# Hybrid decoder layer on one core: branch gates and projections turned token-major, seven-product pairs in gates and output projection, a normalised operand, one set of slots

## The chip, the core and the metric

The kernel runs on one NeuronCore of one Trainium2 chip. The time is device microseconds of one execution. The core has five engines with queues of their own, each worked off in order: TensorE (PE, matmuls; its weight loads are shown as PEld), VectorE (DVE), ScalarE (ACT), GpSimd (POOL) and SyncE (SP, which here only issues transfers). Matmul results land in PSUM accumulators, operands lie in SBUF, weights come from memory by DMA.

## The reference

One layer of a causal decoder, 256 tokens, width 2048, all in float32:

```python
h  = rmsnorm(x, norm1_g)
z  = h @ w_in                    # FoX q,k,v,forget; mLSTM q,k,v,o,i,f; gates ga, gm
a_out = forgetting_attention(rmsnorm(fq), rmsnorm(fk), fv, log_sigmoid(ff + bias))  # 8 heads of 128
m_out = rmsnorm(mlstm_chunkwise(mq, mk, mv, mi, log_sigmoid(mf))) * sigmoid(mo)     # 4 heads
merged = sigmoid(ga) * (a_out @ w_proj_a) + sigmoid(gm) * (m_out @ w_proj_m)
x  = x + merged @ w_out
h2 = rmsnorm(x, norm2_g)
u  = causal_dwconv3(h2 @ w_up)   # 2 x 5632 channels
x  = x + (silu(u_gate) * u_val) @ w_down
```

## The kernel before

Every product is made of three matmuls in a rounded float32 format: an operand is split into a rounded high half and the rest (`put` for activations, `wh`/`wl` for weights), and high x high, low x high and high x low are added up in PSUM. The weights stream through: SP loads chunks of 1 MB into three `raw` buffers (`load_chunk`, L106), ACT rounds half a chunk (a "sub") into `wh` (L138), DVE subtracts it into `wl` (L139), three buffers of each. `next_sub` hands out the next sub and prepares one or two ahead.

Products come in two forms. `block_b` (token-major) keeps 128 tokens x 512 channels in an accumulator: the activation block is the stationary operand, 512 weight columns move; per k-tile and per 128 tokens three matmuls of 512 columns. `block_a` (channel-major) keeps 128 channels x 512: the weight block is stationary and the activation moves, high and low halves side by side in one 512-wide matmul, then a 256-wide one for `wl`; `halves_added` then adds the two halves of the accumulator.

The stages follow each other on PE: `mog` (forget, input and output gates of the heads; three column blocks, mog0 and mog1 together in four accumulators of the pool `acc`, mog2 in the pool `aux`), `fq`, `fk`, `fv`, `mq`, `mk`, `mv`, the branch gates `g`, the projections `p`, `wo`, `up`, and w_down (accumulators `q` and `p`). `mog` to `g` multiply hT, the input times norm1_g only; the norm factor r1 (one number per token) is found while mog2 runs and is applied to the results, as a scale in token-major blocks and as a row tile `rb` in channel-major ones. `gate_evac` (L332, L336) empties the mog accumulators: sums for the gates on DVE, the sigmoid of the output gate into `og` on ACT. `g` and `p` are channel-major, so p's output can be split into the operand mT directly; `wo` is token-major.

w_down already uses pairs of k-tiles as 2x2 blocks: a plain pair ("p") is 8 block products of 3 matmuls, a pair "S" needs 7, for which DVE forms sums of weight blocks (`sums`, L123, L130, L133) and of activation blocks (`sv`, L729 to L732), and results are combined at the end (L811).

Small work (norms, attention steps) stands in a list `tasks`, which the blocks call between subs; the framework then sets the final order on each engine. The scratch `pools` matter for this change: a tile waits until its slot is free. Before, SBUF had eight slots of 8 KB (`a8`), three of 16 KB (`r16`) and one of 8 KB for `og`.

## Time and profile before

| | before |
|---|---|
| runs, median of 3 | 1405.78 us (1405.47 to 1405.92) |
| the profiled execution | 1395.04 us, span 1393.3 us |
| PE / PEld busy | 1384.7 / 1188.5 us (99% / 85%) |
| DVE / ACT / POOL busy | 995.3 / 759.1 / 60.1 us (71% / 54% / 4%) |
| memory traffic | 274.2 MB, 197 GB/s mean |
| g stage to its end, in the chain | until 487.76 us |
| p stage | 487.76 to 576.50 us |
| up stage begins | 666.49 us |

The span runs from the first instruction to the last; the profiled execution's time is a little longer. Busy shares are means over stages with different limits. The chain of waits is followed back from the last instruction; what stands in it sets the end, and what does not is hidden behind it. A row of the groups of instructions reads: line, engine, operation, output<-inputs, shapes, count | busy us, mean ns of one | idle time before them and who ended it. A row of the timeline or the chain starts with its start and its length in us. A row of the windows reads: stretch, length, then busy us and count for PE, PEld, DVE, ACT, POOL, granted PE clock, DMA share, GB/s.

### The profile page before, as it was taken

To read this page: it belongs to the slowest core of one execution; us is meant where nothing else is said; L and a number is where in the kernel's file an instruction comes from. 1 tells how busy PE (TensorE), PEld (TensorE's weight loads), DVE (VectorE), ACT (ScalarE), POOL (GpSimd) and SP (SyncE) were. 2 spreads that over 40 slices of the span, in tenths; PEclk is the share of its full clock that TensorE was granted. 3 is DMA by queue.
4 is the path that set the end of the run, shared out by engine and by line. 5 is a ranking of instruction groups with operands and counts; after the bars stand their busy time and mean duration, and the time that the engine had idled before them with its cause. 6 is when DMAs were issued, how large, how long until landed. Compare 5 with 4: busy or idle time off the path is not lost.

```text
span 1393.3 us, 19175 instructions
## 1 busy us (share of the span) xinstructions
PE 1384.7 (99%) x7347; PEld 1188.5 (85%) x7347; DVE 995.3 (71%) x1448; ACT 759.1 (54%) x1122; POOL 60.1 (4%) x92
## 2 busy tenths in 40 slices
PE   9999999999999999999999999999999999999998
PEld 8988888888888888888888888888888887878877
DVE  8556555556655577655788888888888877886886
ACT  7655544456644455555655565655656554653553
POOL 7001000000000011100000000000000000000000
PEclk9999999999999999999999999999999999999999
DMA  7645554444555555555555555555555657557553
GB/s 259 234 157 189 191 189 152 153 176 150 219 193 197 182 185 201 189 212 197 196 196 196 193 199 209 191 192 203 211 193 183 242 191 268 215 183 269 204 190 121
DMA packets 42491, 274.20 MB, mean 197 GB/s; under 512 B 4832, under 2 KB 4848, under 8 KB 11552
## 3 DMA queue, kind: packets, MB, share of 16 engines
q1 hardware_dynamic: 39168, 260.20, 52.2%
q0 software_dynamic: 3088, 12.77, 2.4%
q8 instruction: 57, 0.93, 0.3%
q14 instruction: 34, 0.28, 0.1%
q10 hardware_dynamic: 144, 0.02, 0.0%
HBM read 265.63 MB, written 7.34 MB: 196 GB/s over the span
## 4 chain that ended last, share of the span: by engine, by line
PE 98%; DMA 1%; DVE 1%; ACT 0%; issue 0%; POOL 0%; DVEq 0%; ACTq 0%
PE up L178 35%; PE q L178 12%; PE g L178 12%; PE p L178 10%; PE wo L178 6%; PE mog L178 3%; PE fq L178 3%; PE mv L178 3%; PE fk L178 3%; PE fv L178 3%; PE mk L178 2%; PE mq L178 2%; DMA raw<-in_w_dn 1%; PE ps_s L178 1%; PE ps_o L178 0%; PE ps_n L178 0%
## 5 line engine op out<-in xcount | busy, mean ns | idle before, releaser
L138 ACT ACTIVATE wh<-raw 128x1024 fp32r<-128x1024 f32 (+2 forms) x496 | 512.2, 1033 | 539.2 <-PE up L178 120.6
L139 DVE TENSOR_TENSOR wl<-raw,wh 128x1024 fp32r<-128x1024 f32 (+2 forms) x496 | 590.1, 1197 | 296.2 <-ACT wh L138 291.3
L178 PE MATMUL up<-h,wh 128*128 128x512 f32 x1408 | 488.6, 392 | 0.0
L178 PE MATMUL up<-h,wl 128*128 128x256 f32 x1408 | 394.8, 281 | 0.0
L178 PEld LDWEIGHTS up<-h,wh 128*128 128x128 f32 x1408 | 263.5, 187 | 57.3 <-DVE h L168 0.2
L178 PEld LDWEIGHTS up<-h,wl 128*128 128x128 f32 x1408 | 266.7, 189 | 0.1
L178 PE MATMUL g<-hT,wh 128*128 128x512 f32 x512 | 180.0, 397 | 0.0
L178 PE MATMUL q<-wh,ghl 128*128 128x512 f32 x512 | 156.3, 390 | 0.0
L178 PE MATMUL g<-hT,wl 128*128 128x256 f32 x512 | 142.5, 278 | 0.0
L178 PEld LDWEIGHTS g<-hT,wh 128*128 128x128 f32 x512 | 96.1, 188 | 21.7
L178 PEld LDWEIGHTS q<-wh,ghl 128*128 128x128 f32 x512 | 96.1, 188 | 20.2
L178 PE MATMUL q<-wl,ghl 128*128 128x512 f32 x256 | 97.9, 391 | 0.6 <-DVE wl L139 0.6
L178 PEld LDWEIGHTS g<-hT,wl 128*128 128x128 f32 x512 | 96.4, 188 | 0.1
L178 PE MATMUL p<-am,wh 128*128 128x512 f32 x256 | 88.8, 394 | 0.0
L703 DVE SCALAR_TENSOR_TENSOR t<-u,cst,t 128x256 f32<-128x256 f32 x176 | 84.8, 482 | 3.7 <-ACT t L701 0.7
L178 PE MATMUL wo<-wh,mT 128*128 128x512 f32 x256 | 79.5, 392 | 0.0
L178 PE MATMUL p<-am,wl 128*128 128x256 f32 x256 | 71.1, 278 | 0.0
L178 PEld LDWEIGHTS p<-am,wh 128*128 128x128 f32 x256 | 48.0, 188 | 11.1
L178 PEld LDWEIGHTS q<-wl,ghl 128*128 128x128 f32 x256 | 47.4, 188 | 11.9 <-DVE wl L139 1.4
L139 DVE TENSOR_TENSOR wl<-sums,wh 128x1024 fp32r<-128x1024 f32 x32 | 39.1, 1223 | 24.7 <-ACT wh L138 24.7
L178 PEld LDWEIGHTS wo<-wh,mT 128*128 128x128 f32 x256 | 47.6, 188 | 9.6
L138 ACT ACTIVATE wh<-sums 128x1024 fp32r<-128x1024 f32 x32 | 33.9, 1061 | 38.2 <-PE q L178 38.2
(237 smaller groups left out, 1655.4 us busy)
## 6 DMA issues: line engine op xcount, KB each, us to landing
raw<-in_w_up SPq DMA_DIRECT2D x88, 1024.0 KB, 4.8
raw<-in_w_dn SPq DMA_DIRECT2D x44, 1024.0 KB, 4.8
raw<-in_w_g SPq DMA_DIRECT2D x32, 1024.0 KB, 4.8
raw<-in_w_fox SPq DMA_DIRECT2D x24, 1024.0 KB, 4.8
raw<-in_w_p SPq DMA_DIRECT2D x16, 1024.0 KB, 4.8
raw<-in_w_out SPq DMA_DIRECT2D x16, 1024.0 KB, 4.8
raw<-in_w_mqk SPq DMA_DIRECT2D x8, 1024.0 KB, 4.8
raw<-in_w_mv SPq DMA_DIRECT2D x8, 1024.0 KB, 4.8
```

The source lines that it names most:

```text
L138: nc.scalar.activation(wh[:, :n], src, AF.Copy)
L139: nc.vector.tensor_tensor(wl[:, :n], src, wh[:, :n].bitcast(F32), ALU.subtract)
L178: nc.tensor.matmul(out, lhsT, rhs, start=start, stop=stop)
L703: nc.vector.scalar_tensor_tensor(out=t, in0=u[:, i : i + S], scalar=w[i], in1=t, op0=ALU.mult, op1=ALU.add)
```

## The change

- hT is used by `mog` only. A second operand hN, the input times norm1_g times `rb`, is made in eight tasks `normalised` (two k-tiles each), issued in the mog2 block and all of them before `gate_evac`. `fq` to `g` multiply hN, and the factor r1 or `rb` falls away from their results. For three pairs of k-tiles the tasks also make the activation sums of the S pairs (`gs`).
- `g` is token-major: four blocks of 1024 columns, the first plain, the other three with three S pairs of eight (`s_block`, which w_down now uses too). The results of the S products are combined in `late` steps, two per sub; the sigmoid is taken block by block.
- `p` is token-major; DVE multiplies by the gates and adds. The sums are then turned by transposes (`merged_pair`), split into mT, and for two pairs the activation sums of `wo` are made.
- `wo` is two blocks of 1024 columns with two S pairs of eight. The transposes of x2 for `h2` stand after the second block; the first two `up` blocks are taken in halves.
- The attention outputs are split when they are made; all large tiles come from 15 slots of 8 KB; `up` accumulates in `aux`; the accumulators of w_down swap pools accordingly.

The core of the diff:

```diff
+PLAIN = "p" * 8
+G_PAIRS = "pSpSpSpp"
+WO_PAIRS = "pSpSpppp"
...
+    def a8(name, shape, dtype=F32):
+        return big.tile([P, *shape], dtype, tag="a8", bufs=15, name=name)
...
+    add_pairs(a["w_g"], [PLAIN] + [G_PAIRS] * 3)
+    add_b(a["w_p"], 512)
+    add_pairs(a["w_out"], [WO_PAIRS] * 2)
+    n = len(subs_of)
+    add_b(a["w_up"], 512)
+    subs_of[n + 1], subs_of[n + 2] = subs_of[n + 2], subs_of[n + 1]
...
+    def put_pair(pair, src):
+
+        put(pair[:, :, 0, :], pair[:, :, 1, :], src.rearrange("p (k s) -> p k s", k=2))
+
+    def put_sums(src, dst, keep):
+
+
+
+        a11, a21, a12, a22 = (src[:, i * P : (i + 1) * P] for i in range(4))
+        n = 4 if keep else 3
+        sv = scratch("sv", [P, n * P])
+        s2, s3, s4 = (sv[:, i * P : (i + 1) * P] for i in range(3))
+        s1 = sv[:, 3 * P :] if keep else a21
+        nc.vector.tensor_tensor(s3, a21, a11, ALU.subtract)
+        nc.vector.tensor_tensor(s1, a21, a22, ALU.add)
+        nc.vector.tensor_tensor(s2, s1, a11, ALU.subtract)
+        nc.vector.tensor_tensor(s4, a12, s2, ALU.subtract)
+        put(dst[0], dst[1], sv)
...
+    def s_block(name, pairs, s_ops, pattern, pools, dst, add=True, per_piece=0):
+
+
+        q = [[pools[0](f"{name}q{tok}{h}") for h in range(2)] for tok in range(2)]
+        ps, late, left = {}, [], pattern.count("S")
+        n_s = left
...
+        def piece():
+            w = next_sub(3)
+            for _ in range(min(2, len(late))):
+                late.pop(0)()
+            run_tasks(per_piece)
+            return w
+
+        def tt(o, x, y):
+            late.append(lambda: nc.vector.tensor_tensor(o, x, y, ALU.add))
...
+            s1, s2, s3, s4 = s_ops[m]
+            w = piece()
+            prod(ps[1], op(0, 0), w, 0, first, last)
+            prod(q[0][1], s4, w, 1, False, False)
+            prod(q[0][0], op(1, 0), piece(), 0, False, False)
+            w = piece()
+            prod(ps[5], s1, w, 0, first, last)
+            prod(ps[7], s3, w, 1, first, last)
+            w = piece()
+            prod(ps[6], s2, w, 0, first, last)
+            prod(q[1][0], op(1, 1), w, 1, False, False)
...
+                late.append(lambda: nc.scalar.activation(c11, ps[1], AF.Copy))
+                tt(u2, c11, ps[6])
+                tt(c21, u2, ps[7])
+                tt(c12, u2, ps[5])
+                tt(c22, c21, ps[5])
+        for f in late:
+            f()
+        return q
...
+    hN, hN_pairs = operand("hN")
+    g_sums = [m for m, kind in enumerate(G_PAIRS) if kind == "S"]
+    g_ops = {}
+
+    def normalised(m):
+        v = scratch("hv", [P, 512])
+        for i in range(2):
+            k = 2 * m + i
+            nc.vector.scalar_tensor_tensor(
+                out=v[:, i * S : (i + 1) * S], in0=xT[k], scalar=cst[:, C_G1 + k : C_G1 + k + 1],
+                in1=rb, op0=ALU.mult, op1=ALU.mult,
+            )
+        put_pair(hN_pairs[m], v)
+        if m in g_sums:
+            i = g_sums.index(m)
+            if i % 2 == 0:
+                g_ops["tile"] = a8(f"gs{i}", [2, 2, 512], F32R)
+            t = g_ops["tile"][:, i % 2]
+            put_sums(v, (t[:, 0], t[:, 1]), True)
+            g_ops[m] = [
+                (t[:, 0, c * P : (c + 1) * P], t[:, 1, c * P : (c + 1) * P]) for c in (3, 0, 1, 2)
+            ]
+
     tasks.extend([lambda: norm(r1), lambda: as_rows(r1)])
-    z2 = block_b("mog2", hT, KD, MOG[2], pool=aux_tile)
+    tasks.extend([lambda m=m: normalised(m) for m in range(KD // 2)])
+    z2 = block_b("mog2", hT, KD, MOG[2], per_chunk=2, pool=aux_tile)
+    run_tasks(len(tasks))
     gate_evac([x[0] for x in z], MOG[0], 0, NG)
     gate_evac([x[1] for x in z], MOG[1], MOG[0] - NG, 0)
     gate_evac(z2, MOG[2], MOG[0] + MOG[1] - NG, 0)
...
     gates = []
-    for g in range(2):
-        gt = big.tile([P, KD, S], F32, tag="r16", bufs=3, name=f"gate{g}")
-        for j in range(KD):
-            t = halves_added(block_a(f"g{g}{j}", hT))
-            nc.vector.tensor_tensor(gt[:, j, :], t, rb, ALU.mult)
+    for b in range(4):
+        gt = a8(f"gate{b}", [2, 1024])
+        pools = (acc_tile, aux_tile) if b % 2 == 0 else (aux_tile, acc_tile)
+        dst = lambda tok, h, gt=gt: gt[:, tok, h * 512 : (h + 1) * 512]
+        q = s_block(f"g{b}", hN_pairs, g_ops, G_PAIRS if b else PLAIN, pools, dst, False, 2)
+        if b == 0:
+            run_tasks(len(tasks))
+        for h in range(2):
+            for tok in range(2):
+                v, z = dst(tok, h), q[tok][h]
+                if b:
+                    nc.vector.tensor_tensor(v, v, z, ALU.add)
+                nc.scalar.activation(v, v if b else z, AF.Sigmoid)
         gates.append(gt)
...
+    def merged_pair(m, ms):
+
+        ps = (aux_tile if m < 6 else acc_tile)(f"ps_m{m}")
+        for i in range(2):
+            for tok in range(2):
+                c = (2 * m + i) % 4 * P
+                nc.tensor.transpose(
+                    ps[:, i * S + tok * P : i * S + (tok + 1) * P], ms[tok][:, c : c + P], ident
+                )
+        if m not in wo_sums:
+            put_pair(mT_pairs[m], ps)
+            return
+        v = scratch("mv", [P, 512])
+        nc.scalar.activation(v, ps, AF.Copy)
+        t = wo_tile[:, wo_sums.index(m)]
+        put_sums(v, (t[:, 0], t[:, 1]), False)
+        put_pair(mT_pairs[m], v)
+        wo_ops[m] = [(mT_pairs[m][:, 0, 0, P:], mT_pairs[m][:, 0, 1, P:])] + [
...
+            z = block_b(f"p{g}{b}", am, 8, 512, k0=8 * g)
+            for tok in range(2):
+                gt = gates[2 * g + b // 2][:, tok, c]
+                if g == 0:
+                    nc.vector.tensor_tensor(ms[tok], z[tok], gt, ALU.mult)
+                else:
+                    t = scratch("mt", [P, 512])
+                    nc.vector.tensor_tensor(t, z[tok], gt, ALU.mult)
+                    nc.vector.tensor_tensor(ms[tok], ms[tok], t, ALU.add)
+        tasks.extend([lambda m=m, ms=ms: merged_pair(m, ms) for m in (2 * b, 2 * b + 1)])
...
+        if b == 1:
+            late_tasks = list(tasks)
+            tasks.clear()
+        q = s_block(f"wo{b}", mT_pairs, wo_ops, WO_PAIRS, pools, dst, True, 1 - b)
+        if b == 1:
+            for f in late_tasks:
+                f()
...
+    ups = [aux_tile(f"up{i}") for i in range(2)]
+    half_a(ups[0], h2, 0, 2)
     tasks.extend([norm2, lambda: as_rows(r2)])
-    ups.append(block_a("up1", h2))
+    half_a(ups[1], h2, 0, 2)
+    half_a(ups[0], h2, 1)
+    half_a(ups[1], h2, 1)
```

Where instructions stand now. ACT's queue while mog2 ends, before: `wh` are weight halves, `og` the output gate's sigmoids from the mog accumulators, `ge` and `gl` steps of the forget gates.

```order
L138 ACTIVATE wh_587<-raw_529 128x692
L336 ACT_TABLE_LOAD
L336 ACTIVATE og<-mog_0_180,r_175 128x346
L336 ACTIVATE og<-mog_1_182,r_175 128x346
L138 ACTIVATE wh_611<-raw_529 128x692
L336 ACTIVATE og<-mog_0_179,r_175 128x332
L336 ACTIVATE og<-mog_1_181,r_175 128x332
L365 ACT_TABLE_LOAD
L365 ACTIVATE ge<-gc 128x24
L321 ACTIVATE rb<-ps_rb 128x256
```

And with the change (`hN` and `gs` are the high halves of the normalised operand and of its sums; `hv` the normalised value):

```order
L158 ACTIVATE wh_769<-raw_632 128x1024
L184 ACTIVATE gs_624<-sv 128x512
L158 ACTIVATE wh_785<-raw_683 128x1024
L184 ACTIVATE hN_530<-hv 128x2x256 x2
L184 ACTIVATE gs_727<-sv 128x512
L184 ACTIVATE hN_531<-hv 128x2x256 x2
L464 ACT_TABLE_LOAD
L464 ACTIVATE og<-mog_0_180,r_176 128x332
L464 ACTIVATE og<-mog_1_182,r_176 128x332
L464 ACTIVATE og<-mog_0_181,r_176 128x346
L464 ACTIVATE og<-mog_1_183,r_176 128x346
```

The sigmoids of the first four accumulators stood among the weight halves of mog2; they now stand behind the first three weight halves of fq (128x1024) and behind the last hN.

DVE's queue in the same place, before:

```order
L318 TENSOR_SCALAR dg<-ident,r_175 128x128 x2
L139 TENSOR_TENSOR wl_588<-raw_529,wh_587 128x692
L332 SCALAR_TENSOR_TENSOR g_178<-mog_0_179,r_175,rows 128x16
L332 SCALAR_TENSOR_TENSOR g_178<-mog_1_181,r_175,rows 128x16
L362 SCALAR_TENSOR_TENSOR gc<-g_178 128x24
L139 TENSOR_TENSOR wl_612<-raw_529,wh_611 128x692
L366 TENSOR_SCALAR gu<-ge 128x24
L369 SCALAR_TENSOR_TENSOR gc<-gu,ge 128x24
L139 TENSOR_TENSOR wl_628<-raw_569,wh_627 128x692
L372 RECIPROCAL gu<-gu 128x24
```

And the last part of what now stands there, after rows of the same kinds for the pairs of k-tiles before:

```order
L483 SCALAR_TENSOR_TENSOR hv<-xT_79,cst,rb 128x256 x4
L185 TENSOR_TENSOR hN_530<-hv,hN_530 128x2x256
L212 TENSOR_TENSOR sv<-hv 128x128
L185 TENSOR_TENSOR hN_530<-hv,hN_530 128x2x256
L213 TENSOR_TENSOR sv<-hv 128x128
L483 SCALAR_TENSOR_TENSOR hv<-xT_79,cst,rb 128x256
L214 TENSOR_TENSOR sv<-sv,hv 128x128
L483 SCALAR_TENSOR_TENSOR hv<-xT_79,cst,rb 128x256
L215 TENSOR_TENSOR sv<-hv,sv 128x128
L483 SCALAR_TENSOR_TENSOR hv<-xT_79,cst,rb 128x256 x2
L185 TENSOR_TENSOR gs_727<-sv,gs_727 128x512
L185 TENSOR_TENSOR hN_531<-hv,hN_531 128x2x256 x2
```

Between two weight halves stood the forget gates' small steps; now the normalised values, their low halves and the sums of all eight pairs stand there, and the first weight half that follows the last of them is the second one of fq (`wl_770`).

PE at the transition from wo to up, before (`ps_h` are transposes of x2, `up` the up-projection):

```order
L178 MATMUL up_5910<-h_5257,wh_5872 128x512
L178 MATMUL up_5910<-h_5257,wl_5873 128x256
L657 MATMUL ps_h_5933<-ident,x_5252 128x128 x4
L657 MATMUL ps_h_5942<-ident,x_5252 128x128 x4
L178 MATMUL up_5910<-h_5258,wh_5913 128x512
L178 MATMUL up_5910<-h_5258,wl_5914 128x256
```

With the change, the end of wo and the first of the transposes:

```order
L219 MATMUL wo1q_5140<-wl_5378,mT_4135 128x512
L219 MATMUL wo1q_5140<-wh_5394,mT_4135 128x512 x2
L219 MATMUL wo1q_5140<-wl_5395,mT_4135 128x512
L837 MATMUL ps_h_5444<-ident,x_4787 128x128
L837 MATMUL ps_h_5444<-ident,x_4788 128x128
```

And the last of them, with up's first products:

```order
L837 MATMUL ps_h_5581<-ident,x_4787 128x128
L837 MATMUL ps_h_5581<-ident,x_4788 128x128
L219 MATMUL up_5512<-h_4792,wh_5412 128x512
L219 MATMUL up_5512<-h_4792,wl_5413 128x256
L219 MATMUL up_5512<-h_4792,wh_5412 128x512
```

Before, six of the eight groups of transposes stood inside wo and the last two behind half an up block; now all eight stand between wo and up, 32 transposes in a row.

More of the change, by code (lines that the diff above doesn't have):

```diff
@@ L113, in split_sub @@
         if j < KD:
-            put(hT[j][:, 0, :], hT[j][:, 1, :], xT[:, j, :], cst[:, C_G1 + j : C_G1 + j + 1])
+            put(hT[j][:, 0, :], hT[j][:, 1, :], xT[j], cst[:, C_G1 + j : C_G1 + j + 1])
         n = 512 if kind == "b21" else chunks[i][1] // 2
-        raw = raws[i]
+        raw, sums = raws[i], s_tiles.get("sums")
         if kind == "whole":
@@ new lines, in s_block, with prod, op @@
+    def s_block(name, pairs, s_ops, pattern, pools, dst, add=True, per_piece=0):
+        q = [[pools[0](f"{name}q{tok}{h}") for h in range(2)] for tok in range(2)]
+        ps, late, left = {}, [], pattern.count("S")
+        n_s = left
+        def prod(out, x, w, c, first, last):
+            wh, wl = w[0][:, c * 512 : (c + 1) * 512], w[1][:, c * 512 : (c + 1) * 512]
+            mm(out, x[1], wh, first, False)
+            mm(out, x[0], wh, False, False)
+            mm(out, x[0], wl, False, last)
+        def piece():
[6 more added lines that the diff above has]
+            late.append(lambda: nc.vector.tensor_tensor(o, x, y, ALU.add))
+        for m, kind in enumerate(pattern):
+            def op(i, tok):
+                t = slice(tok * P, (tok + 1) * P)
+                return pairs[m][:, i, 0, t], pairs[m][:, i, 1, t]
+            if kind == "p":
+                last = m == len(pattern) - 1
+                ws = [piece(), piece()] if last else []
+                todo = (
+                    [(i, tok, h) for h in range(2) for tok in range(2) for i in range(2)] if last
+                    else [(i, tok, h) for i in range(2) for h in range(2) for tok in range(2)]
+                )
+                for i, tok, h in todo:
+                    if i == len(ws):
+                        ws.append(piece())
+                    prod(q[tok][h], op(i, tok), ws[i], 1 - h, m == 0 and i == 0, last and i == 1)
+                continue
+            first, last = left == n_s, left == 1
+            left -= 1
+            if first:
+                ps = {i: pools[1](f"{name}p{i}") for i in (1, 5, 7, 6)}
+            s1, s2, s3, s4 = s_ops[m]
[9 more added lines that the diff above has]
+            prod(q[1][0], op(1, 1), w, 1, False, False)
+            if not last:
+                continue
+            c11, c12, c21, c22 = (dst(tok, h) for tok in range(2) for h in range(2))
+            u2 = scratch("u2", [P, 512])
+            if add:
+                u3 = scratch("u3", [P, 512])
+                late.append(lambda: nc.scalar.activation(u2, ps[1], AF.Copy))
+                tt(c11, c11, ps[1])
+                tt(u2, u2, ps[6])
+                tt(u3, u2, ps[7])
+                tt(u2, u2, ps[5])
+                tt(c21, c21, u3)
+                tt(u3, u3, ps[5])
+                tt(c12, c12, u2)
+                tt(c22, c22, u3)
+            else:
[7 more added lines that the diff above has]
+        return q
@@ L646, in trunk @@
+    x2 = [a8(f"x2{tok}", [D]) for tok in range(2)]
     xs = dram.tile([P, 2, D], F32, name="xs")
     for tok in range(2):
-        nc.gpsimd.dma_start(x2[:, tok, :], a["x"][tok * P : (tok + 1) * P, :])
-    h2 = operand("h2")
+        nc.gpsimd.dma_start(x2[tok], a["x"][tok * P : (tok + 1) * P, :])
+    h2, _ = operand("h2")
     ss2 = const.tile([P, 2, 4], F32, name="ss2")
     def transposed(k):
-        ps = aux_tile(f"ps_h{k}")
+        ps = (aux_tile if k < KD // 2 else acc_tile)(f"ps_h{k}")
@@ L679, in norm2 @@
         rsqrt_mean(r2, ss, D, v)
-    g_pairs = []
-    for n, tag, bufs in ((2, "a8", 8),) * 4 + ((4, "r16", 3),) * 3 + ((2, "og", 1),):
-        t = big.tile([P, n, 2, 512], F32R, tag=tag, bufs=bufs, name=f"ghl{len(g_pairs)}")
-        g_pairs += [t[:, i] for i in range(n)]
+    g_tiles, g_pairs = operand("ghl", NF)
     s_dram = dram.tile([P, N_S * 6 * P], F32R, name="s_dram")
@@ L821, in trunk @@
-        for tok in range(2):
-            for h in range(2):
-                v = xr[:, tok, h * 512 : (h + 1) * 512]
+        dst = lambda tok, h, xr=xr: xr[:, tok, h * 512 : (h + 1) * 512]
+        q = s_block(f"y{b}", g_pairs, y_ops, Y_PAIRS, pools, dst)
+        for h in range(2):
+            for tok in range(2):
+                v = dst(tok, h)
                 nc.vector.tensor_tensor(v, v, q[tok][h], ALU.add)
```

244 lines of the change are left out of this document (92 added, 152 removed).

## The prediction

> **What bounds the kernel now.** I read the page first (busy shares, then the chain of waits), then the groups of instructions by form for the cost of one of each, the chain in order of time for the length of each stage, and last the timeline around the end of the `mog` products, where the change puts new work.
>
> ```profile
> span 1393.3 us, 19175 instructions
> PE 1384.7 (99%) x7347; PEld 1188.5 (85%) x7347; DVE 995.3 (71%) x1448; ACT 759.1 (54%) x1122; POOL 60.1 (4%) x92
> PE 98%; DMA 1%; DVE 1%; ACT 0%; issue 0%; POOL 0%; DVEq 0%; ACTq 0%
> ...
> 92.04 10.93 PE fq L178 x48
> ...
> 365.72 122.03 PE g L178 x704
> 487.76 88.75 PE p L178 x512
> ...
> 632.39 0.44 PE ps_h L657 x4
> ```
>
> PE is 98% of the chain: nearly every microsecond is a matmul following a matmul, so a stage is worth what its matmuls cost back to back, and a stall anywhere on PE is paid in full. The last four rows are such stretches in the chain: token-major products cost 10.93/48 = 0.2277 us each, of which the 24 of one pair of k-tiles take 5.45 us; channel-major products (`g`, `p`) cost 122.03/352 = 0.3467 us per pair of one 512-wide and one 256-wide matmul; four transposes cost 0.44 us.
>
> **What the change takes from PE.** Gates: before 512 pairs x 0.3467 = 177.5 us. After, block 0 is 8 x 24 matmuls and the other three are 5 x 24 + 3 x 21, together 741, x 0.2277 = 168.7 us: -8.8. Projections: 88.75 us becomes 384 x 0.2277 = 87.4: -1.3. Output projection: 384 token-major matmuls become 2 x (6 x 24 + 2 x 21) = 372: 12 x 0.2277 = -2.7. Added: merged operands come out token-major and are turned by eight groups of four transposes, 8 x 0.44 = +3.5. Sum on PE: **-9.3 us**.
>
> **The seven-product pairs.** They do not keep PE quite full, as w_down shows, where they exist already. One S pair and one plain pair are 21 + 24 = 45 matmuls, 10.25 us; these rows are one such period apart:
>
> ```profile
> 1178.76 5.27 PE q L178 x23
> ...
> 1189.11 5.28 PE q L178 x23
> ...
> L139 DVE TENSOR_TENSOR wl<-raw,wh 128x1024 fp32r<-128x1024 f32 x456 | 555.2, 1224 | 288.5 <-ACT wh L138 283.8 <-PE ps_km L178 2.4 <-PE ps_s L178 1.6
> ...
> L123 DVE TENSOR_TENSOR sums<-raw 128x1024 f32<-128x1024 f32 x16 | 19.6, 1226 | 5.1 <-DMA raw<-in_w_dn 4.7
> ...
> L133 DVE TENSOR_TENSOR sums<-raw,sums 128x512 f32<-128x512 f32 x16 | 11.0, 689 | 0.0
> ...
> 1168.00:1278.00 110.00, 109.48 (x476) 88.01 (x477) 90.55 (x97) 58.03 (x60) 0.03 (x1) 1.00 0.57 204
> ```
>
> The period is 10.35, 0.1 over the products. DVE needs for it five 1024-wide `wl` (6.1 us), one 512-wide (0.69), one 1024-wide sum (1.23) and two 512-wide (1.38): 9.4 of 10.35 us. The window row says the same of that whole stage: PE busy 109.48 of 110, DVE 90.55. The gates and w_out get 9 + 4 such pairs, 13 x 0.1 = +1.3. On top, each of the three gate blocks with S pairs sends eight 512-wide combinations and additions (5.5 us) through DVE; over its eight pairs that makes 3 x 7.0 + 5 x 2.45 + 5.5 = 38.8 us of 41.7 us of PE, so the cover is nearly used up. I add 0.2 per block change, five in all: +1.0. Bounds: 0 (in the window row w_down loses 0.5 us over ten such periods) and +10 (2 us a block, if the combinations land beside an S pair).
>
> **Smaller seams.** (a) The mLSTM tasks are issued two per 2.7 us piece instead of one per 2.8 us; a chain through DVE, ACT and POOL already stops PE there for 0.66 us (last row below: 30.34 busy of 31.00), and I put 0.5 more. (b) At p to wo the last pair of merged operands waits for two multiplications and two additions of 0.69 us on DVE; 9 matmuls cover part: +0.7. (c) At wo to up, eight groups of transposes stand in one block (before, two of them):
>
> ```profile
> 655.56 10.93 PE wo L178 x48
> 666.49 2.81 PE up L178 x16
> 669.30 0.87 PE ps_h L657 x8
> 670.17 8.51 PE up L178 x48
> 678.68 0.43 PE ps_rb L178 x2
> ...
> L703 DVE SCALAR_TENSOR_TENSOR t<-u,cst,t 128x256 f32<-128x256 f32 x176 | 84.8, 482 | 3.7 <-ACT t L701 0.7
> ...
> 335.00:366.00 31.00, 30.34 (x178) 26.53 (x177) 20.78 (x45) 20.08 (x38) 1.60 (x3) 1.00 0.42 148
> ```
>
> The transposes only move (3.5 us on PE in either order); but now DVE makes all 16 low halves of h2 (x 0.48 = 7.7 us) with one addition and three `wl` (0.69 + 3 x 1.22) after wo's end, 12.1 us, against 3.5 + 32 x 0.3467 = 14.6 us of PE. They arrive in the order of use: +1.0, from 0 to +4. Together (a) to (c): +2.2.
>
> **The mog to fq seam decides the sign.** Before, fq started behind mog with no gap, since the four accumulators of mog0/mog1 were emptied (L336) in the middle of mog2, and its operand hT was there:
>
> ```profile
> 43.34 0.16 DVE L289 TENSOR_SCALAR v<-ps_norm 128x2 f32<-128x2 f32 x1 [0.71 <-PE ps_norm L178]
> 44.33 0.48 DVE L318 TENSOR_SCALAR dg<-ident,r 128x128 f32<-128x128 f32 x2 [0.83 <-POOL r L290]
> 44.73 0.88 DVE L139 TENSOR_TENSOR wl<-raw,wh 128x692 fp32r<-128x692 f32 x1
> 45.52 0.37 DVE L332 SCALAR_TENSOR_TENSOR g<-mog,r,rows 128x16 f32<-128x16 f32 x2
> ...
> 53.51 2.36 DVE L139 TENSOR_TENSOR wl<-raw,wh 128x1024 fp32r<-128x1024 f32 x2
> ...
> 43.64 1.28 ACT L336 ACT_TABLE_LOAD   x1
> 44.94 0.99 ACT L336 ACTIVATE og<-mog,r 128x346 f32<-128x346 f32 x2
> ...
> 48.89 0.37 ACT L321 ACTIVATE rb<-ps_rb 128x256 f32<-128x256 f32 x1
> ...
> 55.10 0.63 PE L178 MATMUL fq<-wh,hT 128*128 128x512 f32 x2
> ...
> L139 DVE TENSOR_TENSOR wl<-raw,wh 128x692 fp32r<-128x692 f32 x8 | 7.0, 880 | 5.7 <-ACT wh L138 5.7
> ...
> L729 DVE TENSOR_TENSOR sv<-gv 128x128 f32<-128x128 f32 x8 | 2.3, 293 | 0.3
> L165 DVE TENSOR_TENSOR ghl<-gv,ghl 128x512 fp32r<-128x512 f32 x22 | 15.1, 685 | 0.0
> L164 ACT ACTIVATE ghl<-gv 128x512 fp32r<-128x512 f32 x22 | 13.9, 631 | 3.2 <-DVE gv L721 3.2
> ```
>
> After, ACT's queue holds the sigmoids L464 behind the last high half of hN3, and that waits on DVE for the last of 16 products `hv`. fq0's two accumulators are those of mog0_0 and mog0_1, so its first matmul waits for the first sigmoid, whatever operand it needs. DVE can begin `hv` when rb is there: dg ends at 44.81, the matmul ps_rb and ACT's copy of it (0.4 each) give 45.7; wl and g16 (the four rows at 43.34 to 45.52, which stay) end at 45.9. From there, up to the last `hv`, DVE's queue has 16 `hv` x 0.48 = 7.7, six low halves of hN x 0.685 = 4.1, twelve sums x 0.29 = 3.5, two low halves of sums 1.4, three 692-wide wl 2.6, one 1024-wide 1.2: 20.5 us, so 66.4. Neighbours overlap (two wl take 2.36, not 2.45), some 0.07 on each of 40, so 63.6 is the other end; I take 65.0. Then ACT's half (0.63), the table load (1.28) and the first sigmoid (0.55; two take 0.99): fq starts at 67.5 instead of 55.1, **+12.4** (11 to 14). The same queue makes the last wl of mog2 late, which is inside this number: mog2 ends near 58, and PE stands for some 9 us. Behind the sigmoids the forget-gate chain (two more table loads) is late too, but PE has four pieces of fq, 10.9 us, before it asks for it.
>
> The restart is the last term. These are the first products of the program:
>
> ```profile
> 8.79 0.78 PE L178 MATMUL mog<-wh,hT 128*128 128x348 f32 x2
> 9.37 0.78 PE L178 MATMUL mog<-wl,hT 128*128 128x348 f32 x2
> 9.95 1.09 PE L178 MATMUL mog<-wh,hT 128*128 128x348 f32 x4
> ...
> 11.20 0.80 PE L178 MATMUL mog<-wh,hT 128*128 128x348 f32 x4
> 11.83 0.48 PE L178 MATMUL mog<-wl,hT 128*128 128x348 f32 x2
> 12.15 0.80 PE L178 MATMUL mog<-wh,hT 128*128 128x348 f32 x4
> ```
>
> Until 9.95 us two follow each other in 0.58 us, later six in 0.95: 0.29 against 0.158 us each, although the page's granted clock reads full. From 6.3 to 9.95 that costs some 12 x 0.135 = 1.6 us. No gap later in this trace is over about a microsecond, so whether a 9 us stand brings it back is not shown: 0 to 1.6, and I take 1.6, since the start is the nearest case of a PE that had stood.
>
> The Trainium skill (TensorE: Matmul & The Clock Gate, section "Part 1: The HAM clock gate") says that PE drops to half clock after an idle window of about 3.4 us and needs about that long of work to return. The trace agrees on the return (3.6 us at about half rate). By that rule the stand costs an estimated 1.7 us, and without it the sum would be 1.6 lower.
>
> **Sum**: -9.3 + 1.3 + 1.0 + 2.2 + 12.4 + 1.6 = **+9.2 us**. The profiled execution before took 1395.0 us (span 1393.3), so the profiled one after should take about 1404; the runs' median, 1405.8, lies 10.7 above that execution, and I add the same 9.2 to it: **1415 us**, +0.65%. Up and w_down keep their products, tiles and order; their accumulators swap pools, which changes nothing where PE never waited for them.
>
> **Rivals.** (1) *Faster: the seam does not hold fq.* If the sigmoids were out of the way early, fq would wait only for hN0, ready before mog2 ends, and the loss would be the late wl alone, about 3 us: -9.3 + 4.5 + 3 = -1.8; and with block changes and seams at their lower bounds (0 rather than 3.2), -5.0: 1401. For it: before, these same sigmoids ran at 44.94, ten microseconds ahead of fq, so nothing but their place in the queue holds them. Against it: that place, and fq0's need of those very accumulators. It decides if the seam costs less than 4.8 us (9.3 - 4.5). Chance 0.09. (2) *No change*: DVE's small operations run shorter than their means, the seam costs 3 to 7 us and the restart nothing: within 3 us of 1405.8. Chance 0.06. (3) *DVE becomes the bound in the gates*: 38.8 of 41.7 us leaves 7%, and order within a block matters; 2 us a block over five blocks in place of my 1.0 gives 1424. For it: the DVE sums. Against: w_down runs the same pairs at 10.35. Chance 0.12. (4) That the change does not do what it says can be left out: the order on PE holds the 741 matmuls of the gates. Forecast: 0.73.
>
> **Range.** The forecast's own range is 1409 to 1419 (seam 11 to 14, restart 0 to 1.6, wo to up 0 to 4). With the rivals' shares, 8 in 10 lie in 1407 to 1421. About 0.2%, 2.8 us, is what a measurement of this kernel tells from no change; by the cases, faster 0.09, same 0.07, slower 0.84.
>
> **What would show it.** In the profile after: fq's first matmul at 66 to 69 us, released by ACT `og`, with PE idle from about 58; before that, one wait of mog2 for DVE wl of 2 to 3 us; the first ten products of fq at twice 0.23 us; gates ending in about 170 us from their start, plus the mLSTM's few; S pair and plain pair 10.3 to 10.5 us apart; 14 to 17 us from the end of wo to up2. I am wrong if fq starts before 60, if ACT's sigmoids stand there before the last `hv`, or if PE shows more than 10 us of waits on DVE wl between gates and w_out.

## The result

The changed kernel takes 1421.24 us (median of 4, 1420.93 to 1421.42), the kernel before 1405.62 us beside it (1404.79 to 1405.92): ratio 1.0112, 95% interval 1.0094 to 1.0129, or +15.6 us. The forecast was 1415 us, +9.2, with 1407 to 1421 as range: the direction was right, the size too small, and the end of the range missed by a quarter of a microsecond.

The page of the changed kernel, that is the summary of its profiled execution (span, busy times, granted clock in 40 slices, the chain's shares):

```profile
span 1419.7 us, 18391 instructions
...
PE 1388.6 (98%) x6956; PEld 1167.0 (82%) x6956; DVE 1049.3 (74%) x1474; ACT 756.3 (53%) x1085; POOL 45.5 (3%) x76
...
PEclk8989999999999999999999999999999999999999
...
PE 95%; DVE 2%; DMA 2%; ACT 1%; issue 0%; POOL 0%; SPq 0%; ACTq 0%; DVEq 0%
```

PE has 6956 matmuls instead of 7347, yet is busy 4 us longer, and the chain, 98% PE before, now holds 5% of other things. The clock row has two dips that it did not have. PE's waits show where it stood ahead of them (engine and line, what it waited for, total us, times, longest):

```profile
PE mog L219 <- DVE hT L188: 10.1, 1, 10.1
PE fq L219 <- ACT og L464: 8.4, 1, 8.4
PE y0q L219 <- DVE wl L159: 2.2, 1, 2.2
...
PE mog L219 <- DVE wl L159: 1.4, 1, 1.4
```

Before, the same view had nothing over 1.2 us. The chain in order of time shows where they stand, and stages further on:

```profile
15.32 36.12 PE mog L219 x216
...
74.54 13.89 PE fq L219 x48
...
419.09 5.44 PE g2q L219 x24
...
429.60 5.26 PE g2q L219 x23
...
439.95 5.25 PE g2q L219 x23
...
460.89 5.44 PE g3q L219 x24
...
679.48 3.49 PE ps_h L837 x32
...
694.96 483.26 PE up L219 x2735
```

The first product of the program starts at 15.32 us (6.32 before), fq at 74.54 (55.10); the four rows of `g2q` and `g3q` belong to the gates' seven-product blocks; and the last row is up from its third block on: 483.26 us, where the same 2735 matmuls took 474.14. From the first product of a stage to the first of the next, the two profiled executions compare so (us):

| stage | before | after | difference | forecast |
|---|---|---|---|---|
| until the first mog product | 6.3 | 15.3 | +9.0 | 0 |
| mog | 48.8 | 59.2 | +10.4 | +12.4 |
| fq | 47.7 | 50.5 | +2.8 | +1.6 |
| fk to mv | 194.3 | 194.3 | 0 | 0 |
| g | 190.6 | 183.3 | -7.3 | |
| p, wo, up but for its pace | 668.3 | 669.4 | +1.1 | g to up: -4.8 |
| up's pace | | | +9.1 | 0 |
| w_down to the end | 237.3 | 238.7 | +1.4 | 0 |

Together that is the 26.4 us by which the spans differ, but the runs differ by 15.6. The kernel before has two times: of its 87 executions in this study 21 took 1404 to 1406 us (the four of the result among them) and 66 took 1394 to 1397, its profile too. So the 10.7 us that lay between its profile and its runs were not an offset around the span; experiments 7 to 10 look for what they were. Without up's pace the spans differ by 17.3 us. The 1.7 us between that and 15.6 are within the 2 us or so by which executions of one time scatter, and were not traced further.

### The profile page after: what moved, and what is told of

Read it like the earlier page. It is cut to its first block, busy times and chain, and to the rows that moved or that the text cites. A ratio compares the mean times of both kernels' runs of the same rounds, so it can differ in the third digit from the quotient of the medians.

```text
span 1419.7 us, 18391 instructions
## 1 busy us (share of the span) xinstructions
PE 1388.6 (98%) x6956; PEld 1167.0 (82%) x6956; DVE 1049.3 (74%) x1474; ACT 756.3 (53%) x1085; POOL 45.5 (3%) x76
## 4 chain that ended last, share of the span: by engine, by line
PE 95%; DVE 2%; DMA 2%; ACT 1%; issue 0%; POOL 0%; SPq 0%; ACTq 0%; DVEq 0%
PE up L219 35%; PE y1q L219 6%; PE p L219 6%; PE y0q L219 6%; PE fq L219 3%; PE mv L219 3%; PE fk L219 3%; PE fv L219 3%; PE wo0q L219 3%; PE mog L219 3%; PE wo1q L219 3%; PE g0q L219 2%; PE g1q L219 2%; PE g2q L219 2%; PE g3q L219 2%; PE y0p L219 2%
## 5 line engine op out<-in xcount | busy, mean ns | idle before, releaser
L219 PE MATMUL p<-wh,am 128*128 128x512 f32 x256 | 79.5, 391 | 0.0
L219 PE MATMUL y0q<-wh,ghl 128*128 128x512 f32 x256 | 78.1, 390 | 0.0
L219 PE MATMUL y1q<-wh,ghl 128*128 128x512 f32 x256 | 78.0, 390 | 0.0
L219 PEld LDWEIGHTS y1q<-wh,ghl 128*128 128x128 f32 x256 | 48.0, 188 | 10.1
L219 PEld LDWEIGHTS y0q<-wh,ghl 128*128 128x128 f32 x256 | 48.0, 188 | 10.1
L219 PEld LDWEIGHTS p<-wh,am 128*128 128x128 f32 x256 | 47.6, 188 | 9.7
L887 ACT ACTIVATE t<-u,cst 128x256 f32<-128x256 f32 x88 | 52.0, 591 | 1.5 <-DVE u L884 1.4
L219 PE MATMUL y0q<-wl,ghl 128*128 128x512 f32 x128 | 49.0, 391 | 2.2 <-DVE wl L159 2.2
L219 PE MATMUL p<-wl,am 128*128 128x512 f32 x128 | 49.9, 390 | 0.0
L219 PE MATMUL y1q<-wl,ghl 128*128 128x512 f32 x128 | 48.8, 390 | 0.0
```

The costliest lines, as they stand in the source:

```text
L219: nc.tensor.matmul(out, lhsT, rhs, start=start, stop=stop)
L887: nc.scalar.activation(t, u[:, 2:], AF.Identity, scale=w[2], bias=w[3])
```

## The experiments

**1. The kernel before once more.** No edit.

> The kernel before, profiled a second time. Its first profile took 1395.04 us, its timed runs 1405.6, and the profile after shows up 9.1 us longer (483.26 against 474.14 us for 2735 matmuls) although no line of up's products changed. Theory A: up's slower pace (0.3534 against 0.3488 us per pair of matmuls) belongs to the execution and not to the change; then this profile shows up at 482 to 484 us and a span of 1402 to 1406, with the first product still at 6 to 7 us and fq still at 55 to 56. Theory B: the pace belongs to the changed kernel; then up stays at 474 here, and the 10.7 us between the first profile and the timed runs lie elsewhere, for instance in a start as late as after (15 us).

Four executions: 1394.65, 1395.07 (the profiled one), 1404.78, 1405.59. The profile is like the first, with up still at 474:

```profile
678.79 474.14 PE up L178 x2735
```

The profile shows theory B's numbers, and no late start either. That doesn't settle it: the profile fell on the shorter time again, and what makes the longer one is not in it. The question goes on in experiments 7 to 10.

**2. The start, held to program order.** The edit puts each operation named behind the one traced before it on its engine:

```diff
+        pin = tc.keep_in_program_order if j < KD else (lambda x: x)
+        pin(nc.scalar.activation(wh[:, :n], src, AF.Copy))
+        pin(nc.vector.tensor_tensor(wl[:, :n], src, wh[:, :n].bitcast(F32), ALU.subtract))
...
+            tc.keep_in_program_order(nc.scalar.activation(sq, x, AF.Square))
...
+        tc.keep_in_program_order(nc.scalar.activation(t, x, AF.Square))
```

> The changed kernel, with ACT and DVE held to program order in the mog products, so that hT of a k-tile comes ahead of the squares of all later ones; nothing else. Theory A: the first product at 15.32 us instead of 6.32 is the change's, because ACT has eight squares (and so four transfers of xT) ahead of the first hT; then the first product starts at 6.5 to 8.5 us here, TensorE's granted clock shows no half in the first 20 us, and the time falls by 7 to 9 us, to 1412 to 1414. Theory B: the late start is one of the execution; then the time stays within 1.5 us of 1421.2.

1412.25 us (4 runs, 1411.62 to 1413.81): 9.0 less. ACT's first rows in the changed kernel (timeline: start and length in us, what ended the wait ahead):

```profile
4.48 0.42 ACT L428 ACTIVATE sq<-xT 128x256 f32<-128x256 f32 x1 [1.81 <-DMA xT<-in_xT]
...
6.96 0.71 ACT L431 ACTIVATE t<-xT 128x256 f32<-128x256 f32 x2
...
13.05 0.72 ACT L431 ACTIVATE t<-xT 128x256 f32<-128x256 f32 x2 [1.83 <-DMA xT<-in_xT]
13.68 3.69 ACT L187 ACTIVATE hT<-xT,cst 128x256 fp32r<-128x256 f32 x9
```

The same view with the order held:

```profile
4.47 0.51 ACT L188 ACTIVATE hT<-xT,cst 128x256 fp32r<-128x256 f32 x1 [1.80 <-DMA cst<-in_cst]
5.17 0.78 ACT L159 ACTIVATE wh<-raw 128x694 fp32r<-128x694 f32 x1 [0.19 <-DMA raw<-in_w_mog]
5.86 0.49 ACT L188 ACTIVATE hT<-xT,cst 128x256 fp32r<-128x256 f32 x1
```

In the changed kernel the square of the first k-tile and those of the next seven (`sq`, `t`) come ahead of the first hT. The last two need the fourth transfer of xT, which lands at 13 us, so the first hT, which needs only the first transfer of xT, waits for four. In order, hT starts at 4.47 us and PE at 6.00. Theory A.

**3. Only the slots of xT, in the kernel before.** This came last, to find what had changed the order. It makes two tiles of xT, as the change does, and takes them from the slots of hT.

```diff
-    xT = big.tile([P, KD, S], F32, tag="r16", bufs=3, name="xT")
+    xts = [big.tile([P, 8, S], F32, tag="a8", bufs=8, name=f"xT{i}") for i in range(2)]
+    xT = [xts[k // 8][:, k % 8] for k in range(KD)]
```

> The kernel before, with one part of the change alone: xT lies in two of the 8 KB slots from which hT is taken too, instead of one 16 KB slot of its own. Theory A: this alone makes the order on ACT put the squares ahead of the first hT, and so costs the start what it cost the changed kernel; then the first product starts at 14 to 16 us instead of 6.3, and the time rises by 8.5 to 10 us over the kernel before, to about 1405 (or 1414 in executions with the slow rhythm in up). Theory B: the late start came from the 15 slots, the normalised operand or the mog2 tasks as well; then the first product starts under 8 us and the time stays within 2 us of 1395.9 (or 1405.4).

Four executions, 1404.77, 1404.79, 1413.42 and 1413.91, beside 1395.51 for the kernel before: +9.3 on its shorter time, and some +8 on the longer (1405.4 in other experiments). The chain starts its products as late as the changed kernel does:

```profile
14.52 36.83 PE mog L178 x216
...
687.49 474.14 PE up L178 x2735
```

So the part of "one set of slots" that moves xT had the price: with xT in two tiles from the slots of hT, and nothing else changed, the planner (the part of the framework that sets the final order) orders ACT otherwise. Whether the shared slots do it or the two tiles, and why, was not tried.

**4. The seam: sigmoids ahead of the normalised operand.**

```diff
+    tasks.append(lambda: gate_evac([x[0] for x in z], MOG[0], 0, NG))
+    tasks.append(lambda: gate_evac([x[1] for x in z], MOG[1], MOG[0] - NG, 0))
     tasks.extend([lambda m=m: normalised(m) for m in range(KD // 2)])
...
-    gate_evac([x[0] for x in z], MOG[0], 0, NG)
-    gate_evac([x[1] for x in z], MOG[1], MOG[0] - NG, 0)
```

> The changed kernel, with the sigmoids of the first two mog blocks issued ahead of the normalised operand instead of behind it. Theory A (as predicted): their place in ACT's queue holds fq, 8.4 us, and the stand brings the half clock back (2.9 us in fq's first 48 matmuls); then PE stands under 3 us, fq starts at 62 to 65 us, and the time falls by 9 to 13 us, to 1408 to 1412. Theory B: DVE's queue holds fq as well, since its 20 us of work for the operand stand ahead of fq's weights; then fq starts near 63 but its second piece waits for DVE wl until about 70, and the time falls by 2 to 6 us, to 1415 to 1419.

1418.11 us (4 runs, 1416.78 to 1419.53): 3.1 less, theory B. fq's accumulators are free early now, fq starts 50.3 us behind mog's first product (59.2 unedited), and PE then stands 6.6 us for the weights of its next ones (PE's waits):

```profile
PE fq L219 <- DVE wl L159: 6.6, 1, 6.6
```

The chain of the same kernel, up to the products that waited:

```profile
73.16 0.68 DVE hN L185
73.84 1.15 DVE wl L159
...
75.03 8.89 PE fq L219 x32
```

The chain ahead of 75.03 is DVE without a break: `gs` and `hN` for the last k-tiles, and only behind them this `wl`. Two queues held fq, each until about the same time (ACT until 74.5 us in the changed kernel, DVE until 75.0 here); taking one away shows the other.

**5. fq back on hT, the normalised operand made during fq.** The edit of experiment 4, and:

```diff
+    n8 = [lambda m=m: normalised(m) for m in range(KD // 2)]
+    tasks.extend([gates_a, n8[0], gates_b, n8[1], gates_c, *n8[2:]])
...
-        qk_evac(block_b(f"fq{b}", hN, KD, 512), qT, b, C_QG, FD**-0.5, "q")
+        qk_evac(block_b(f"fq{b}", hT, KD, 512, per_chunk=2), qT, b, C_QG, FD**-0.5, "q", True)
```

> As the run before, and fq takes hT again and is scaled by r1 behind the product, as in the kernel before; the 20.5 us of DVE work for the normalised operand are spread over fq's 44 us instead of standing between mog and fq. Theory A: the seam's whole price goes, and DVE has room in fq (16 wl are 20 us of 44); PE stands under 1 us between mog and fq, fq takes 44 to 45.5 us, and the time falls by 11 to 14 us, to 1407 to 1410. Theory B: DVE gets too full in fq, PE waits there for wl by 3 to 6 us in all, and the time falls by 6 to 9 us, to 1412 to 1415.

1408.84 us (4 runs, 1407.29 to 1411.19): 12.4 less, theory A. No wait stands between mog and fq, and in fq's 46 us PE is full while DVE takes the work in: 37.34 us busy. The window over fq:

```profile
64.00:110.00 46.00, 45.92 (x211) 36.80 (x211) 37.34 (x73) 27.48 (x46) 2.02 (x2) 1.00 0.52 182
```

In fq of the kernel before, DVE is busy for 26.67 of 45 us:

```profile
55.00:100.00 45.00, 45.00 (x208) 36.35 (x207) 26.67 (x44) 22.10 (x36) 2.02 (x2) 1.00 0.54 197
```

**6. The half clock alone.** 30 matmuls, whose result is not used, fill the stand between mog and fq in the changed kernel:

```diff
+    ps_fill = aux_tile("ps_fill")
+    fill = hT[0].rearrange("p l s -> p (l s)")
+    for _ in range(30):
+        tc.keep_in_program_order(nc.tensor.matmul(ps_fill, fill[:, :P], fill, start=True, stop=True))
```

> The changed kernel, with 30 matmuls of 512 columns (30 x 0.2277 = 6.8 us, their result is not used) between the last mog product and fq, where PE stood 8.4 us. Theory A: the stand is what brought the half clock, and it cost 2.9 us in fq's first 48 matmuls (13.89 against 10.93 us); then fq starts at the same time, its first 48 take 10.9 to 11.2 us, no window behind 25 us shows less than full clock, and the time falls by 2 to 3 us, to 1418 to 1419.5. Theory B: the slow start of fq is one of its supply (wh and wl come late); then fq's first 48 stay at 13 us or more and the time within 1 us of 1421.2.

Three executions at 1418.8 to 1419.4 and one at 1410.0. The three say -2.2, theory A; the fourth lies 9 us lower, as up's other pace would make it (experiment 8), but it was not the one profiled. The windows across the stand in the changed kernel (the granted clock is the third number from the end):

```profile
66.00:67.00 1.00, 0.19 (x2) 0.00 (x0) 1.00 (x3) 0.88 (x1) 0.00 (x0) 0.86 0.68 229
67.00:74.00 7.00, 0.00 (x0) 0.00 (x0) 7.00 (x17) 4.44 (x8) 0.00 (x0) 0.50 0.26 109
...
80.00:81.00 1.00, 1.00 (x5) 0.79 (x4) 0.20 (x1) 0.98 (x2) 0.00 (x0) 0.81 0.00 0
```

The same stretch, filled:

```profile
65.00:70.00 5.00, 5.00 (x25) 4.26 (x24) 5.00 (x13) 2.33 (x3) 0.00 (x0) 1.00 0.60 210
70.00:75.00 5.00, 3.45 (x15) 2.54 (x15) 5.00 (x9) 4.51 (x8) 0.00 (x0) 1.00 0.00 0
```

fq's first 48 matmuls fall from 13.89 to 11.21 us at the same start (74.54 and 74.04). So of fq's +2.8 the clock is nearly all.

**7. Both repairs** (2 and 5 together).

> Two repairs of the changed kernel together: ACT and DVE in program order in the mog products (9.0 us measured alone) and fq on hT with the normalised operand made during fq (12.4 us measured alone). Theory A: the two stand at different places and add up: 1421.2 - 9.0 - 12.4 = 1399.8, from 1398 to 1402, with up still at 483 us. Theory B: they overlap, because DVE and ACT are the scarce engines of the whole mog stage and an earlier start only finds them busy later; then 1403 to 1407.

Ten executions: eight at 1400.4 to 1403.6, two at 1390.68 and 1391.54. The eight, with a median of 1401.5, are theory A's 1399.8 with 1.7 lost; the two are not foreseen by either theory. The profile fell on one of the two, and there up takes 474.14 us, as in the kernel before, where theory A expected 483. So this kernel has two times as well, and their distance, 10 us, is that of the kernel before.

**8. The rhythm of up.** PE's rows around ps_rb (timeline: start, length), the last disturbance ahead of up's 1376 pairs of a 512-wide and a 256-wide matmul. The kernel before:

```profile
678.76 0.59 PE L178 MATMUL up<-h,wh 128*128 128x512 f32 x1
679.19 0.28 PE L178 MATMUL up<-h,wl 128*128 128x256 f32 x1
679.30 0.39 PE L178 MATMUL up<-h,wh 128*128 128x512 f32 x1
...
679.65 0.39 PE L178 MATMUL up<-h,wh 128*128 128x512 f32 x1
```

The changed kernel, the same place:

```profile
694.61 0.58 PE L219 MATMUL up<-h,wh 128*128 128x512 f32 x1
695.03 0.28 PE L219 MATMUL up<-h,wl 128*128 128x256 f32 x1
695.15 0.40 PE L219 MATMUL up<-h,wh 128*128 128x512 f32 x1
...
695.51 0.40 PE L219 MATMUL up<-h,wh 128*128 128x512 f32 x1
...
695.86 0.40 PE L219 MATMUL up<-h,wh 128*128 128x512 f32 x1
...
696.21 0.40 PE L219 MATMUL up<-h,wh 128*128 128x512 f32 x1
```

From wide matmul to wide matmul: 0.35, 0.35 before, all alike (0.347 on the mean: 474.14 us over 1367.5 pairs). After: 0.36, 0.35, 0.35, and so on; in the trace's nanoseconds 361, 349, 350, over and over to the end of up (0.3534 on the mean). Ahead of ps_rb the kernel before runs in a third rhythm (350 and 343 in turn, or 345 and 348 counted from narrow to narrow), the changed one already in that of three lengths; the first step behind ps_rb, from a wide matmul to a narrow one, is 0.425 us in the one and 0.420 in the other. Each piece has the same instructions in the same order, and the granted clock reads 1.00 throughout. The edit exchanges two matmuls:

```diff
+        todo = [(q, i) for q in range(len(ks)) for i in range(2)]
+        if state.get("swap"):
+            todo[1], todo[2] = todo[2], todo[1]
```

> The changed kernel, with two matmuls of every half block of up exchanged: the first two k-tiles go wh, wh, wl, wl instead of wh, wl, wh, wl; same work, same operands. In the profiles so far each pair of a 512-wide and a 256-wide matmul in up takes 0.230 + 0.117 us before, all alike, and after it runs through three lengths, 0.361, 0.349 and 0.350 us, over and over from the first pair to the last. Theory A: this is a rhythm that PE falls into at the start of up and keeps as long as nothing disturbs it; then the exchange, at every eighth pair, breaks it, up falls from 483 to 473 to 477 us, and the time by 6 to 10 us, to 1411 to 1415. Theory B: the pace is set by where the changed kernel's operands lie, or by other engines' traffic; then the exchange changes nothing, up stays within 2 us of 483 and the time within 2 us of 1421.2.

> The kernel before, with the same exchange in up. Its executions fall on two times, about 1395 and 1405.5, ten microseconds apart; both profiles of it fell on the shorter one and show up at 474. Theory A: the longer one is the slower rhythm in up, entered by chance; then with the exchange all executions here lie within 3 us of one another, at 1394 to 1399. Theory B: the two times come from somewhere else; then they remain, some 10 us apart.

> Both repairs and the exchange in up. Theory A: 1399.8 - 6 to 10 us, that is 1390 to 1394, faster than the kernel before. Theory B (the exchange does nothing): 1398 to 1402.

Changed kernel: 1415.30 us (4 runs, 1414.85 to 1418.00). Kernel before: 1399.49 us, all ten executions within 1398.81 to 1400.82, while beside it the unedited one took 1394.6 to 1396.6 and, four times in 25, 1404.7 to 1405.4. Both repairs: 1396.51 us, ten within 1394.72 to 1397.81. In all three profiles up takes 478.11 us, halfway between the two paces:

```profile
694.26 478.11 PE up L219 x2735
```

The start times show why halfway: the exchange turns one rhythm into the other, so every first half block runs in the fast one and every second in the slow one. So theory A's mechanism holds: an exchange of two matmuls changes the pace, and the band of the kernel before shrinks to 2.0 us. But its levels supposed that the exchange only mends. They are missed narrowly for the changed kernel (1411 to 1415, up at 473 to 477) and for the kernel before (1394 to 1399), and by 2.5 us for both repairs (1390 to 1394). With the rhythm forced alike, the change costs 1415.30 - 1399.49 = 15.8 us, as in the runs.

**9. One exchange only, and no alternation at all.** The exchange once, in up's fifth block; and in place of it all wide matmuls of a half block first (`todo.sort(key=lambda t: t[1])`).

> Both repairs, and the exchange of two matmuls once only, at the first pairs of up's fifth block. In the runs with the exchange in every half block the slow rhythm (pairs of 0.361, 0.349, 0.350 us) and a fast one (0.345 and 0.349 in turn) followed each other from half block to half block: the exchange turned the one into the other. Theory A: one exchange is kept to the end, so executions that start in the slow rhythm (9 of 10 of the kernel with both repairs, 1401.5) come out at about 1391.5 to 1393, and those that start in the other may turn slow. Theory B: the slow rhythm comes back by itself within a few blocks; then the times stay at 1401.

> Both repairs, and in every half block of up the eight 512-wide matmuls first and the eight 256-wide ones behind them, so that two lengths do not alternate and no rhythm can form. Theory A: each matmul then costs its width plus a fixed part, (0.227 + 0.120) x 1386 pairs as in the fast rhythm; up2 onward takes 470 to 477 us in every execution, and all times lie within 3 us, at 1390 to 1394. Theory B: eight 256-wide matmuls in a row wait for their weights; then up takes 480 us or more and the time 1397 or more.

> The kernel before, with up grouped in the same way. Theory A: its second time of 1405 is gone and all executions lie within 2 us of 1395.9; so the two kernels can be compared with the rhythm out of the way, and the one with both repairs is 3 to 6 us shorter. Theory B: both times stay.

Once: ten executions, six at 1390.1 to 1395.3 and four at 1401.6 to 1402.5, against two and eight without it. That is too few to call it a cure, and the profile fell on an execution whose up ran at 347 ns ahead of the exchange already: there the exchange turns this into the rhythm of 350 and 343, which stays to the end (474.16 us). That a slow up turns fast for good by one exchange there is not shown. Grouped: both repairs 1400.07 us (1398.42 to 1401.50), kernel before 1402.60 (1399.97 to 1403.87), ten each, one time only; but from the first product behind ps_rb to its last, up takes 480.5 us in both instead of 477.1 in the fast rhythm (486.3 in the slow), and with both repairs w_down waits 5.6 us for DVE wl instead of 1.8 (in the kernel before 2.7 instead of 1.0). One time instead of two was right, the level wrong in both: grouping costs nearly what the slow rhythm does.

**10. The rhythm ahead of ps_rb.** One exchange, in the last half block ahead of ps_rb; in the changed kernel and with both repairs:

```diff
+    state["swap"] = True
     half_a(ups[1], h2, 1)
```

> The changed kernel with one exchange of two matmuls in up, in the last half block ahead of ps_rb, and nothing else. Theory A (the rhythm ahead of ps_rb settles up's pace for good): the exchange turns the slow rhythm there into the two-length one, the step behind ps_rb is 0.425 us, up takes 474 us instead of 483, and most executions come to 1411 to 1413 (9 us under 1421.2), with a few near 1421. Theory B (chance, or where the operands lie): nearly all executions stay at 1419 to 1422.

> Both repairs and the one exchange ahead of ps_rb. Theory A: of ten executions most come to 1390 to 1392 instead of two of ten, so the median falls from 1401.4 to about 1391, under the 1395.9 of the kernel before. Theory B: most stay at 1400 to 1403.

Changed kernel: 1412.56, 1412.88, 1414.69 and 1420.36. Both repairs: eight at 1390.78 to 1393.99 and two at 1402.3 and 1402.4, median 1392.31 us, where the kernel before took 1396.03 beside it (13 of 14 at 1395.4 to 1396.7): ratio 0.999, 95% interval 0.9969 to 1.0010 over both times. Like with like, the eight against the thirteen, it is some 4 us shorter; with the rhythm forced alike it was 3.0 (experiment 8) and 2.5 (experiment 9). Its up:

```profile
674.96 474.14 PE up L220 x2735
```

Theory A. In both traces PE runs at 350 and 343 in turn behind the exchange, where the unedited one runs at 361, 349, 350, and the step behind ps_rb is 0.425 us. Which rhythm PE is in when ps_rb comes settles the 474 or 483 us behind it. The nine traces in which up is unedited say the same without exception: the four with 350 and 343 ahead of ps_rb (the kernel before in both profiles, experiments 3 and 7) have up at 474, the five with 361, 349, 350 (the changed kernel, experiments 2, 4, 5 and 6) at 483. By their times the changed kernel was in the slow one in all its four executions, the kernel before in a quarter of its own. The share of fast executions, eight of ten against two of ten in experiment 7, was taken on another chip than there, with no unedited one of both repairs beside it. That the changed order of up's first half blocks puts PE into the slow rhythm is likely, but was not undone by itself. No profile of the kernel before fell on its longer time, so that this is the slow rhythm is concluded from experiments 8 and 9 (one time, once the rhythm is forced) and the equal distance, not seen.

## Why the prediction was right and wrong

**The step that failed is one that isn't there: the start.** The sum takes mog up to rb as it was, a term put at nothing, and quotes its first products at 8.79 to 12.15 us from the kernel before. That "all large tiles come from 15 slots" could move the first hT was not considered; the order on ACT was read at the seam only, not at the head of the program. Missed: +9.0, shown by experiments 2 (-9.0) and 3 (+9.3). It is more than the whole distance between 9.2 and 15.6: with the start held to its order (1412.25 us), the change costs 6.6 us, so the terms that are in the sum came to 2.6 less than forecast.

**The seam** was the right mechanism. fq's first matmul is released by ACT `og` as forecast; it starts 59.2 us behind the first product, where 61.2 was forecast (67.5 less 6.3). The term, +12.4, measured +10.4. In experiment 2 it is 61.1 us, but only since mog's products wait more there. From the norm's `v` on DVE (43.34 before, 51.82 here) to fq it is 22.7 us in both, against 11.8 before and 24.2 forecast: the seam alone is +11.0, the low end of 11 to 14. The chain ahead of fq:

```profile
68.14 0.60 DVE hN L185
...
70.34 0.40 DVE hv L483
...
70.97 0.63 ACT gs L184
71.60 1.04 ACT hN L184 x2
...
72.66 1.28 ACT L464
```

The last `hv` ends at 71.73, that is 62.7 without the 9.0 us of the late start, where 65.0 was taken: in a row, DVE's operations take 0.40 (`hv`) and 0.60 us (`hN`) and not their means of 0.48 and 0.685, so the bound of 63.6 with overlap was the better choice and still too late. By the chain ACT no longer waits for DVE from 70.95 on: it has three high halves in a row (`gs`, two of `hN`) ahead of the table load, where one was counted, and from the last `hv` to fq it takes 2.8 us instead of 2.5. mog2's wait for DVE wl was 1.4, not 2 to 3.

**Rival 1** said that fq would need only hN0 if the sigmoids were out of the way, with about 3 us left for the late wl. Experiment 4 shows 6.6 us of wait left there: DVE's queue alone holds fq's second weights. So the rival had its price wrong, not only its odds; the whole price goes only if DVE's work leaves the seam (experiment 5).

**The restart** was put at 1.6 us and measured 2.7 to 2.8 in this profile. From the rows at 66 and 80 us above (0.86 and 0.81 of a microsecond's mean) the clock fell to half at 66.7 us and came back at 80.4, 5.8 us into fq; at the start of the program PE had needed 3.6. Three more windows of the changed kernel:

```profile
8.00:9.00 1.00, 0.00 (x0) 0.00 (x0) 1.00 (x1) 0.60 (x1) 1.00 (x2) 0.85 0.93 242
18.00:19.00 1.00, 1.00 (x5) 1.00 (x5) 1.00 (x3) 0.85 (x3) 0.79 (x1) 0.53 0.00 0
63.30:66.70 3.40, 1.52 (x9) 1.24 (x8) 3.40 (x7) 1.66 (x3) 0.00 (x0) 1.00 0.23 48
```

The Trainium skill (TensorE: Matmul & The Clock Gate, "Part 1: The HAM clock gate") says that the gate looks at free-running windows of about 3.4 us. The trace agrees in so far as the two stretches at half clock in the changed kernel, 8.7 to 18.9 and 66.7 to 80.4 us, are 3 and 4 times 3.41; by that grid a restart costs more than one window if work begins inside one. But it fell behind 3.4 us in which PE was busy for 1.52 (last row): not an idle window.

The size was luck either way. In experiment 8's profile of the changed kernel fq starts at the same 74.53, behind the same stand of 8.4 us, and the clock is back at 78.0:

```profile
74.53 12.81 PE fq L219 x48
...
77.00:78.00 1.00, 1.00 (x4) 0.81 (x3) 0.00 (x0) 0.99 (x2) 0.00 (x0) 0.50 0.97 410
78.00:79.00 1.00, 1.00 (x6) 0.77 (x6) 0.36 (x2) 0.20 (x1) 0.00 (x0) 0.99 0.91 385
```

There fq takes 49.4 us, and so it does in experiment 2: 1.7 over the 47.7 before. The grid of 3.41 us fits both: 80.4 less 3.41 is 77.0, so the first whole stretch of work began 2.4 us into fq; 78.0 less 3.41 is 74.6, just behind fq's first product. So one stand costs 1.7 to 2.8 us, by when in fq the clock comes back. The forecast's 1.6, its upper bound too, was read too short from the start of the kernel before: its single matmuls start 0.29 us apart until 10.53, not 9.95, which makes 14 x 0.135 = 1.9 us by the same working.

**PE's own sum** was right. Gates, projections, wo and up together were put at -4.8 (-9.3 + 1.3 + 1.0 + 2.2) and measured -6.2. One S pair and one plain pair are 10.35 us apart (429.60 to 439.95), as forecast, but this is the longest of the block's three periods: the blocks of the gates take 41.8 us against 41.7 of products. So of the 0.1 per S pair and the 0.2 per block change only 0.1 a block came there, and nothing of the worse of rival 3 (2 us a block), although DVE was expected to be nearly full. From the end of wo to up's third block it takes 15.5 us (14 to 17 forecast).

**"Up and w_down keep their products, tiles and order"** was right for the products and wrong for the time: PE comes to up in another rhythm and keeps it (+9.1 in the profile); w_down's +1.4 is mostly one wait of 2.2 us for DVE wl at its head, where it waited 0.6 before. In the runs up's pace cancels, since the longer time was what the kernel before had in all four of them. The forecast added the 10.7 us between its profile and its runs as if they lay outside the span. That this step did no harm was luck: it holds only if both kernels run up at the slow pace, as the changed one did by its trace and the kernel before by its times.

## What to carry to other kernels

Where a change puts tiles into shared slots or hands the order to a planner, read the order of each engine from the first row on: 9 of the 15.6 us here are an order that none of the change's lines mentions. When a wait is traced to one queue, ask what the next queue would hold until when; here two ended close together, and taking one away gained 3 of 12 us. And before a difference between two profiles is put down to a change, compare the pace of products that did not change, and the spread of both kernels' executions.

## What the hardware showed

- A stream that alternates 512-wide and 256-wide matmuls can run in three rhythms: 347 ns a pair, all alike; 350 and 343 in turn; or 361, 349, 350 (353 on the mean). It keeps the one it has, through 1376 pairs and their blocks, until a disturbance (another matmul in between, two of a kind in a row) turns it into another. What inside PE makes them is open.
- Streams of 512-wide matmuls alone run at 0.227 us a matmul in both kernels (fv: 32.69 us for 144), and no profile here shows a second pace.
- The granted clock can fall behind 3.4 us in which PE was busy for 45%, and a stand of 8.4 us then costs 1.7 to 2.8 us more than its own length.
